# Mixer A's values by Strassen's seven products, ahead of its attention, in a two-layer encoder on one core

## The chip, the cores and the metric

The kernel runs on one core of one Trainium2 chip. The metric is the device time of one execution, in microseconds (us); lower is better. The kernel before takes 1451.28 us in the median of 3 runs (1450.83 to 1451.67). The profile is one more execution: 1451.78 us, of which 1449.6 us lie between its first and its last instruction.

Five engines work beside each other, each through its own instructions in a fixed order: TensorE (PE in the profile; its weight loads are PEld), VectorE (DVE), ScalarE (ACT), GpSimd (POOL), and SyncE (SP), which only issues transfers. An engine stops at an instruction whose semaphores have not arrived, and everything behind it on that engine stops too.

## The reference

Two layers on x (512 positions of 1024 numbers, float32). Each layer is x = x + mixer(norm(x)), then x = x + mlp(norm(x)), with mlp(h) = relu(h·w1)²·w2 over 4096 hidden columns. Layer 0's mixer, the one that the change touches:

```python
def dilated_mixer(h, w_qkv, q_gain, k_gain, w_o):
    qkv = (h @ w_qkv).reshape(B, S, 3, N_GROUPS, A_HEADS, A_HEAD_DIM)   # 3 groups, 8 heads of 128
    outs, lses = [], []
    for g, (window, dil) in enumerate(DIL_CONFIGS):     # (128, 1), (512, 4), (2048, 16)
        q = rope(rms_norm(qkv[:, :, 0, g], q_gain[g]), S)
        k = rope(rms_norm(qkv[:, :, 1, g], k_gain[g]), S)
        v = qkv[:, :, 2, g]
        o, lse = dilated_group(q, k, v, window, dil)    # softmax over a dilated window
        outs.append(o); lses.append(lse)
    wts = jax.nn.softmax(jnp.stack(lses, 0), axis=0)
    o = wts[0][..., None] * outs[0]
    for g in range(1, N_GROUPS):
        o = o + wts[g][..., None] * outs[g]
    return o.reshape(B, S, A_WIDTH).astype(h.dtype) @ w_o
```

The values v are thus a plain product of h (512 x 1024) with 3 groups x 8 heads x 128 = 3072 columns of w_qkv. Layer 1 uses multi-head latent attention, which the change does not touch.

## The kernel before

**Matmuls in three passes.** Every float32 operand of a large product is split into a high part (rounded by ACT, `whi` for weights) and a low part (the difference, by DVE, `wlo`), and a product is hi·hi + hi·lo + lo·hi: three matmuls of 128 x 128 by up to 512 columns each. `load_unit` (L145 to L159) loads a piece of weights of 256 rows (`raw`, by SP, L146 or L148), and splits it (ACT L157, DVE L158). `run_block` (L161 to L190) holds the results of four row tiles of 128 positions in four PSUM banks and goes through the units of weights in groups: `[1] * 4` takes one unit at a time for all four tiles, `[4]` all units for one tile and then the next. The matmul is L184. Four pairs of `whi` and `wlo` buffers are shared by the whole program.

**Norm and turn.** `norm_tile` (L204 to L221) scales a tile of x by its root mean square (ACT's square L136, a power on POOL L131, DVE L212) and a gain, turns it by eight transposes on TensorE (L123), and splits it into `hT`.

**Mixer A.** Four pairs of heads, one after the other. For each pair `qk_block` projects queries and keys of group 0, 1 and 2 (512 columns, 192 matmuls each), normalises and rotates them (squares on ACT, then DVE L308, L311, L315, L316), turns them, and computes scores and exponentials (L340 to L362). Then `v_all` runs twice, once per head: `v_block` projects the values of the head's three groups together (384 columns, 96 matmuls of 128x384); group 0's part makes a round trip through DRAM into another order (`v0n`, `v0c`). `merge` (L376 to L417) weighs the three groups, and `pv` (L419 to L446) multiplies with the values. In the last pair one head's values come ahead of the queries and keys. Then `project` (L635) multiplies with `w_o`, after splitting the heads' outputs (L655).

**MLP.** The product with w2 goes in four chunks of 1024 rows; each is a Strassen product (Winograd's form) with seven half-sized products instead of eight: `wino` (L489 to L590). Weight sums are made by transfers that POOL issues and that add to what is in the buffer (accumulates, L509); sums of activations by DVE (L517), split at L485 and L486; the matmul is L580. The table `ORDER` (L588) sets the products' order: 1, 5, 3, 6, 2, 7, 4. Each product takes 24 matmuls of 512 columns.

**What sets the order.** The program is written in the order above, but a scheduler lays each engine's instructions out beforehand by its own estimate of when their inputs are ready: matmuls of one product can be put between those of another. On the chip each engine then keeps that order.

## Time and profile before

| | |
|---|---|
| median of 3 runs | 1451.28 us (1450.83 to 1451.67) |
| the profiled execution | 1451.78 us |
| its span, first to last instruction | 1449.6 us |
| TensorE busy | 1410.4 us, 97% |
| VectorE, ScalarE, GpSimd busy | 887.1, 727.2, 198.4 us |
| moved by SP's queue, by POOL's accumulates | 142.74 MB, 33.56 MB |
| mean granted clock of TensorE | 0.999 |

How to read it: a row of a timeline gives start, duration, engine, line, operation, output<-input with shapes, and in brackets the engine's idle time ahead of it with what ended it. A group's row gives the count, then busy time and the mean in ns, then idle time and its releasers. Durations of matmuls are latencies and overlap; the interval at which they follow each other is read from their starts. A wait row gives what the engine waited for, the total in us, how often, and the longest.

### The profile page before, as it was taken

Reading aid. Unit: us, or ns where it says so; the run is one execution under the profiler, and the core shown is the slowest. Engines: PE = TensorE matmul, PEld = TensorE weight load, DVE = VectorE, ACT = ScalarE, POOL = GpSimd, SP = SyncE. Lnnn points to the kernel's source line nnn. Section 1 sums busy time; section 2 is a strip of 40 time slices with the busy share of each in tenths; the row PEclk is TensorE's granted clock in tenths of the full one; section 3 lists DMA queues with packets and bytes.
Section 4 is the critical chain, followed back from the end, with each engine's and each line's share of the span. In section 5 each row is a group of like instructions: output and inputs, shape, how many; then the busy total and the mean of one; then the engine's idle time right before and its main releaser. Section 6 shows DMA issues by size and latency. Waiting matters only on the chain.

```text
span 1449.6 us, 19315 instructions
## 1 busy us (share of the span) xinstructions
PE 1410.4 (97%) x7116; PEld 1196.8 (83%) x7116; DVE 887.1 (61%) x1421; ACT 727.2 (50%) x1590; POOL 198.4 (14%) x197
## 2 busy tenths in 40 slices
PE   7999999999999999999999999899999999999998
PEld 6889889889988878888888877776768988888877
DVE  6765566566537655266475749788755266475647
ACT  5544455355335533453544545777633454544543
POOL 1120120011011101011020222332101011020210
PEclk9999999999999999999999999999999999999999
DMA  7325114321622344749394853310013749394853
GB/s 228 100 57 162 58 49 129 110 63 45 174 92 62 97 140 141 222 112 236 91 233 127 195 136 66 99 30 30 30 44 136 206 111 239 93 223 138 189 116 88
DMA packets 134813, 177.52 MB, mean 122 GB/s; under 512 B 8768, under 2 KB 73536, under 8 KB 134720
## 3 DMA queue, kind: packets, MB, share of 16 engines
q1 hardware_dynamic: 117312, 142.74, 31.1%
q0 software_dynamic: 17408, 33.56, 14.0%
q8 instruction: 56, 0.92, 0.2%
q14 instruction: 37, 0.30, 0.1%
HBM read 172.07 MB, written 4.19 MB: 122 GB/s over the span
## 4 chain that ended last, share of the span: by engine, by line
PE 89%; ACT 4%; DVE 3%; DMA 2%; issue 1%; POOL 1%; SPq 0%; DVEq 0%; ACTq 0%; POOLq 0%
PE acc L184 58%; PE sc L580 10%; PE tp L580 7%; PE tp L123 4%; PE acc L859 1%; PE acc L835 1%; PE sc L753 1%; PE sco L444 1%; PE sco L440 1%; PE sc L351 1%; PE sc L835 1%; ACT whi L157 1%; ACT junkb L136 1%; DVE wlo L158 1%; PE tp L859 0%
## 5 line engine op out<-in xcount | busy, mean ns | idle before, releaser
L184 PE MATMUL acc<-whi,hT 128*128 128x512 f32 (+2 forms) x1600 | 486.3, 379 | 5.6 <-DVE t L311 2.2
L158 DVE TENSOR_TENSOR wlo<-raw,whi 128x1024 fp32r<-128x1024 f32 (+3 forms) x170 | 195.7, 1156 | 230.5 <-ACT whi L157 229.5
L184 PEld LDWEIGHTS acc<-whi,hT 128*128 128x128 f32 x1600 | 296.2, 189 | 47.3 <-issue 2.9
L184 PE MATMUL acc<-hT_f,whi 128*128 128x512 f32 (+1 forms) x1152 | 319.4, 366 | 1.9 <-DVE resid L641 1.2
L157 ACT ACTIVATE whi<-raw 128x1024 fp32r<-128x1024 f32 (+3 forms) x170 | 170.0, 1005 | 269.0 <-PE acc L184 177.4
L184 PE MATMUL acc<-wlo,hT 128*128 128x512 f32 (+2 forms) x800 | 300.2, 375 | 0.2 <-DVE wlo L158 0.2
L184 PEld LDWEIGHTS acc<-hT_f,whi 128*128 128x128 f32 x1152 | 208.4, 189 | 37.8 <-DVE resid L641 1.6
L524 DVE TENSOR_TENSOR wlo<-wqs,whi 128x1024 fp32r<-128x1024 f32 x112 | 137.3, 1227 | 113.6 <-ACT whi L523 113.5
L184 PE MATMUL acc<-hT_f,wlo 128*128 128x512 f32 (+1 forms) x576 | 205.1, 365 | 0.0
L523 ACT ACTIVATE whi<-wqs 128x1024 fp32r<-128x1024 f32 x112 | 118.6, 1060 | 167.6 <-PE acc L184 66.2
L184 PEld LDWEIGHTS acc<-wlo,hT 128*128 128x128 f32 x800 | 151.2, 189 | 20.5 <-DVE wlo L158 1.1
L580 PE MATMUL sc<-whi,asp 128*128 128x512 f32 x512 | 165.1, 390 | 0.8 <-ACT asp L485 0.8
L509 POOL DMA_DIRECT2D wqs<-in_ffn_w_dram x64 | 77.6, 1350 | 528.4 <-DVE wlo L524 339.9
L184 PEld LDWEIGHTS acc<-hT_f,wlo 128*128 128x128 f32 x576 | 108.6, 189 | 17.5
L131 POOL TENSOR_TENSOR qrs<-rs_v,nhalf 128x4 f32<-128x4 f32 x48 | 61.5, 1290 | 408.3 <-DVE rs_v L128 393.8
L580 PE MATMUL tp<-whi,asp 128*128 128x512 f32 x352 | 112.2, 390 | 2.6 <-DVE asp L486 2.6
L580 PEld LDWEIGHTS sc<-whi,asp 128*128 128x128 f32 x512 | 96.1, 188 | 21.6 <-ACT asp L485 1.6
L580 PE MATMUL sc<-wlo,asp 128*128 128x512 f32 x256 | 99.6, 389 | 0.0
L580 PEld LDWEIGHTS tp<-whi,asp 128*128 128x128 f32 x352 | 65.9, 188 | 17.2 <-DVE asp L486 3.5
L580 PE MATMUL tp<-wlo,asp 128*128 128x512 f32 x176 | 68.5, 389 | 0.0
L136 ACT ACTIVATE junk<-acc 128x128 f32<-128x128 f32 x192 | 53.1, 277 | 18.9 <-PE acc L184 13.8
L554 DVE TENSOR_TENSOR resid<-resid,sc 128x512 f32<-128x512 f32 x64 | 43.0, 682 | 24.4 <-PE sc L580 24.4
(190 smaller groups left out, 1796.3 us busy)
## 6 DMA issues: line engine op xcount, KB each, us to landing
wqs<-in_ffn_w_dram SPq DMA_DIRECT2D x80, 512.0 KB, 5.1
raw<-in_ffn_w_dram SPq DMA_DIRECT2D x64, 512.0 KB, 4.4
wqs<-in_ffn_w_dram POOLq DMA_DIRECT2D x64, 512.0 KB, 7.2
raw<-in_a_w_qkv_dram SPq DMA_DIRECT2D x96, 256.0 KB, 3.4
raw<-in_a_w_qkv_dram SPq DMA_DIRECT2D x64, 192.0 KB, 2.8
raw<-in_a_w_o_dram SPq DMA_DIRECT2D x8, 512.0 KB, 4.0
raw<-in_b_w_o_dram SPq DMA_DIRECT2D x8, 512.0 KB, 3.7
xt<-in_x_dram SPq DMA_DIRECT2D x8, 256.0 KB, 5.7
```

Source lines behind the costliest of these rows:

```text
L123: PE.transpose(o, i, ident)
L131: G.tensor_tensor(out, v[:, :n], nhalf[:, :n], op=ALU.pow)
L136: A.activation(junk, x, AF.Square, scale=1.0 / math.sqrt(dim), accum_out=out)
L157: A.activation(hi[:, :nk, :n], raw[:, :nk, :n], AF.Copy)
L158: V.tensor_tensor(lo[:, :nk, :n], raw[:, :nk, :n], hi[:, :nk, :n].bitcast(F32), op=ALU.subtract)
L184: PE.matmul(accs[o][:, oc], lhsT=lt, rhs=rt, start=(kt == 0 and p_i == 0 and hv == 0), stop=(kt == total - 1 and p_i == 2), skip_group_che ...
L509: nc.gpsimd.dma_start(t, src, accum_op=ALU.add)
L523: A.activation(hi, x, AF.Copy)
L524: V.tensor_tensor(lo, x, hi.bitcast(F32), op=ALU.subtract)
L554: V.tensor_tensor(sl, sl, banks[t], op=op)
L580: PE.matmul(bk[t], lhsT=lt, rhs=rt[:, j], start=(first and k == 0 and i_ == 0), stop=(k == 3 and i_ == 2), skip_group_check=True)
L835: PE.matmul(sc, lhsT=lt, rhs=rt, start=(i == 0), stop=(i == 4))
```

## The change

**Values first.** The work on the values of six heads moves ahead of the attention into a new function `v_phase`. For each group these heads' 768 columns, the 1024 rows and the 512 positions are halved, and seven products take the place of eight: 24 matmuls of 128x384 each. Products of unsummed halves (2 and 1) come first; for group 0 the head numbered 6 is then projected directly, while DVE and ACT make and split the sums of activations (`Ssp`); then 5, 3, 6, 7, 4 (`piece`). The weight operand `bT` is b11 + b12 (DVE), becomes b11 + b12 + b22 for product 6 and that plus b21 for product 4 through accumulates on POOL's queue (L331: 12 transfers of 384 KB). The results go to DRAM (`vall`), and each pair of heads reads its part back (`v_load`). The gain is loaded ahead of x.

**Attention.** The blocks of queries and keys follow one another without values between them, in groups of two units (`[2, 2]`). A pair's softmax end, merge and product with the values stand behind the first block of the next pair. The last head (7) is projected directly behind the last scores (`v_last`), and the first column block of `w_o` is begun between the last two heads' `pv` (`first_cols`).

**MLP.** In the last chunk of each layer the products run in the order 1, 2, 5, 3, 6, 7, 4 (`ORDER_LAST`).

The diff, cut to its core:

```diff
@@ -237,95 +244,322 @@
+        def add_block(t, g, ki, ni):
+            for u in range(2):
+                nc.gpsimd.dma_start(t[:, 2 * u:2 * u + 2], wblk(g, ki, ni, u), accum_op=ALU.add)
...
+        gain_b = gain_table(norm_mix[0:1, :].rearrange("o d -> (o d)"), D, "g_mix0")
+        load_x(0)
+        nc.sync.dma_start(ck[:, 0:P], consts[:, 0:P])
+        b21[0] = block(0, 1, 0, "b21")
+        load_x(1)
+        b11[0] = block(0, 0, 0, "b11")
+        load_x(2)
+        load_x(3)
...
+        def product(p, w, banks, first, u, t):
+            if (p, u) not in parts:
+                split(p, w, u)
+            hi, lo = parts[p, u]
+            for j in range(2):
+                k = 2 * u + j
+                ah, al = A_OF[p](k, 0, t), A_OF[p](k, 1, t)
+                for i_, (lt, rt) in enumerate(((ah, hi), (ah, lo), (al, hi))):
+                    PE.matmul(banks[t][:, :VH], lhsT=lt, rhs=rt[:, j], start=(first and k == 0 and i_ == 0),
+                              stop=(k == 3 and i_ == 2), skip_group_check=True)
...
+        def piece(g, ba):
+            bb = new_banks("b")
+            both(5, bT[g], bb, True)
+            put(g, 1, 1, "set", bb, False)
+            add_block(bT[g], g, 1, 1)
+            both(3, b22[g], bb, False)
+            put(g, 0, 1, "set", bb, False)
+            b3 = vp.tile([P, 4, VH], F32, tag="h32", name=nm("b3"))
+            for u in range(2):
+                us = slice(2 * u, 2 * u + 2)
+                V.tensor_tensor(b3[:, us], b12[g][:, us], b22[g][:, us], op=ALU.add)
+            both(6, bT[g], ba, False)
+            put(g, 0, 1, "sub", ba, True)
+            add_block(bT[g], g, 1, 0)
+            both(7, b3, ba, False)
+            put(g, 1, 1, "sub", ba, True)
+            both(4, bT[g], ba, False)
+            put(g, 1, 0, "set", ba, True)
...
+            both(2, b21[g], bd, True)
+            put(g, 0, 0, "set", bd, False)
+            both(1, b11[g], ba, True)
+            put(g, 0, 0, "add", ba, True)
+            for u in range(2):
+                sum1(g, u)
+            piece(g, ba)
...
+        for b in range(HA // 2):
...
+            vs = v_load(b)
+            for g in range(NG):
+                scores(b, g, qkT, Pt, stats)
+                if g + 1 < NG:
+                    qkT = project_in(b, g + 1)
+            if b + 1 < HA // 2:
+                qkT = project_in(b + 1, 0)
+                finish(b, Pt, stats, vs)
...
+        merge(stats, Pt)
+        v_last(*vs)
+        oA = new_hT()
+        for h in range(HA - 2):
+            split_o(h)
+        pv(HA // 2 - 1, 0, Pt, *vs)
+        first_cols = block_groups(w_units(a_w_o[0], 0, 512), [3, 1], 512, act_stationary(oA, 512))
+        next(first_cols)
+        pv(HA // 2 - 1, 1, Pt, *vs)
...
-        for p, chain, first, (i, n, op) in ORDER:
+        for p, chain, first, (i, n, op) in ORDER if done is None else ORDER_LAST:
...
+    ORDER_LAST = [ORDER[0], ORDER[4]] + ORDER[1:4] + ORDER[5:]
```

**The order on the engines.** First TensorE in the new V phase, group 0: the end of product 5 (operand `Ssp`, banks `tp`), the first two matmuls of product 6 (banks `sc`, weights `whi_549` from the accumulated `bT`), and then product 3.

```order
L422 MATMUL tp_483<-wlo_465,Ssp_111 128x384
L422 MATMUL tp_483<-whi_464,Ssp_111 128x384 x2
L422 MATMUL tp_483<-wlo_465,Ssp_111 128x384
L422 MATMUL tp_483<-whi_464,Ssp_111 128x384
L422 MATMUL sc_157<-whi_549,Ssp_112 128x384 [waits Activation_49]
L422 MATMUL sc_158<-whi_549,Ssp_112 128x384
L422 MATMUL tp_482<-whi_512,Ssp_114 128x384 [waits Activation_49]
L422 MATMUL tp_482<-wlo_513,Ssp_114 128x384 [waits DVE_49]
```

Nothing of this stood here before; product 3 can start only behind the two matmuls of product 6, whose weights wait for the accumulate.

Then POOL at layer 0's last w2 chunk: `wqs` are the chunk's weight buffers (an accumulate each), `cgB` and `sgB` are tables for layer 1. Before:

```order
L509 DMA wqs_5335<-in_ffn_w_dram 128x2x512 [waits DMASW6_49,DVE_49]
L691 TENSOR_TENSOR cgB<-ck,gr 128x4x32 [waits DMAHW6_49,PE_49]
L692 TENSOR_TENSOR sgB<-ck,gr 128x4x32
...
L691 TENSOR_TENSOR cgB<-ck,gr 128x4x32 [waits DMAHW7_49]
...
L509 DMA wqs_5335<-in_ffn_w_dram 128x2x512 [waits DMASW7_49,DVE_49]
L693 TENSOR_SCALAR sgB<-sgB 128x8x32 [waits Pool_49]
L509 DMA wqs_5335<-in_ffn_w_dram 128x2x512 [waits DMASW4_49,DVE_49]
```

And now:

```order
L966 TENSOR_TENSOR cgB<-ck,gr 128x4x32 [waits DMAHW0_49,PE_49]
L967 TENSOR_TENSOR sgB<-ck,gr 128x4x32
...
L966 TENSOR_TENSOR cgB<-ck,gr 128x4x32 [waits DMAHW1_49]
...
L968 TENSOR_SCALAR sgB<-sgB 128x8x32 [waits Pool_49]
L779 DMA wqs_5372<-in_ffn_w_dram 128x2x512 [waits DMASW2_49,DVE_49]
L779 DMA wqs_5372<-in_ffn_w_dram 128x2x512 [waits DMASW3_49,DVE_49]
```

The rows left out are more `cgB` and `sgB` operations: nine in all, the last one being `sgB<-sgB`. Of product 6's two accumulates the first stood ahead of the nine and the second behind eight of them; now both stand behind all nine.

Last TensorE at the same place now: the end of product 5 (banks `tp_7493` and `tp_7494`, operand `asp_7490`), two matmuls of product 6 (`sc`, operand `asp_7571`), then product 3.

```order
L850 MATMUL tp_7494<-wlo_7512,asp_7490 128x512
L850 MATMUL tp_7494<-whi_7511,asp_7490 128x512
L850 MATMUL sc_7411<-whi_7574,asp_7571 128x512 [waits Activation_49]
L850 MATMUL sc_7412<-whi_7574,asp_7571 128x512
L850 MATMUL tp_7493<-whi_7535,asp_7532 128x512 [waits DVE_49]
L850 MATMUL tp_7493<-wlo_7536,asp_7532 128x512
```

Two matmuls of product 6 stand ahead of product 3, as four did before; their weights come from the first of the two accumulates.

More of the change, by code (lines that the diff above doesn't have):

```diff
@@ L174, in run_block @@
                 src, nk, dims = units[ui]
-                loaded.append(load_unit(src, nk, dims, n, (name, ui)))
+                loaded.append(load_unit(src, nk, dims, n, raw=raws[ui] if raws else None))
                 ui += 1
@@ L188, in run_block @@
                     if gi == len(groups) - 1 and hv == halves - 1:
-                        evac(o, accs[o])
+                        yield o, accs[o]
             kt0 = nkt
+            if gi < len(groups) - 1:
+                yield None
+    def run_block(units, groups, n, mm, evac, outs=NT, halves=1):
+        for end in block_groups(units, groups, n, mm, outs, halves):
+            if end is not None:
+                evac(*end)
     def act_stationary(hT, n):
@@ L643, in evac @@
                     norm_tile(r, resid[:, r], gain, hT_n, pool)
+            if c == 0 and begun is not None:
+                for end in begun:
+                    if end is not None:
+                        evac(*end)
+                continue
             run_block(w_units(w, 512 * c, 512), [1, 1, 1, 1] if c == 0 else [4], 512, act_stationary(o_hl, 512), evac)
```

381 lines of the change are left out of this document (266 added, 115 removed).

## The prediction

> **What bounds the kernel now.** I read the page first (who is busy), then TensorE's waits (what its idle time is made of), then a table by stage, and timelines where a stage is touched.
>
> ```profile
> PE 1410.4 (97%) x7116; PEld 1196.8 (83%) x7116; DVE 887.1 (61%) x1421; ACT 727.2 (50%) x1590; POOL 198.4 (14%) x197
> ...
> q1 hardware_dynamic: 117312, 142.74, 31.1%
> q0 software_dynamic: 17408, 33.56, 14.0%
> ```
>
> TensorE is busy for 1410.4 of 1449.6 us. So work taken from it shortens the run one for one, as long as the others keep up, and only 39 us of waiting can be gained or added to. TensorE's waits, with the total, the number and the longest:
>
> ```profile
> PE tp L123 <- DVE xn L212: 9.9, 2, 8.9
> PE tp L580 <- DVE asp L486: 2.6, 2, 1.5
> PE tp L123 <- DVE pT L426: 2.4, 2, 2.1
> PE acc L184 <- DVE t L311: 2.2, 1, 2.2
> PE sc L580 <- ACT asp L485: 0.8, 2, 0.4
> ```
>
> The first row is the start (8.9 us until the first norm is done); the others lie in places that the change touches. By stage (the first 60 us of QK blocks, one pair of heads in steady state, the last pair, the start of w_o):
>
> ```profile
> 30.00:93.00 63.00, 61.43 (x311) 51.38 (x309) 44.69 (x86) 37.08 (x127) 12.70 (x10) 1.00 0.23 69
> ...
> 150.24:273.92 123.68, 123.65 (x702) 111.42 (x702) 75.14 (x143) 60.48 (x190) 14.74 (x12) 1.00 0.30 90
> ...
> 395.84:527.00 131.16, 127.72 (x700) 111.89 (x700) 80.12 (x150) 64.91 (x196) 15.56 (x12) 1.00 0.29 90
> 527.00:580.00 53.00, 50.45 (x311) 44.02 (x310) 26.13 (x36) 17.01 (x27) 4.63 (x6) 1.00 0.42 148
> ```
>
> After the length come TensorE, its weight loads, DVE, ACT and POOL. A steady pair leaves TensorE 0.03 us idle in 123.68: a pure TensorE stage.
>
> **The change part by part.** The sum is made against the profiled execution, 1451.78 us.
>
> *Fewer products.* A V matmul at full and at half clock:
>
> ```profile
> 91.04 0.39 PE L184 MATMUL acc<-whi,hT 128*128 128x512 f32 x1
> 93.67 0.41 PE L184 MATMUL acc<-whi,hT 128*128 128x384 f32 x1 [2.24 <-DVE t L311]
> ...
> 94.09 0.51 PE L184 MATMUL acc<-whi,hT 128*128 128x384 f32 x2
> 94.44 0.33 PE L184 MATMUL acc<-wlo,hT 128*128 128x384 f32 x1
> 94.61 0.51 PE L184 MATMUL acc<-whi,hT 128*128 128x384 f32 x2
> ...
> 96.18 1.16 PE L184 MATMUL acc<-whi,hT 128*128 128x384 f32 x3
> 97.14 0.52 PE L184 MATMUL acc<-wlo,hT 128*128 128x384 f32 x1
> ```
>
> From 94.09 to 94.61 three are issued: 0.173 us each. (0.33 is latency, not the interval.) Six heads took 6 x 96 = 576 such matmuls; three groups by seven products by 24 are 504. **72 x 0.173 = -12.5 us.** All else on TensorE keeps its count.
>
> *The stall at 91.4.* It stood where V's first matmul wanted a bank that QK's evacuation still held; now no V block follows. It cost 2.24 us, and behind it the clock fell: from 96.18 to 97.14 three matmuls take 0.96 us, 0.32 each, for some 3.2 us, of which (0.32 - 0.173)/0.32 = 1.5 is lost. **-3.7** (0 if the same wait comes back behind a QK block).
>
> *The start.* Now the gain is loaded ahead of x, and x's first tile comes last of the two.
>
> ```profile
> 8.87 1.97 PE L123 MATMUL tp<-ck,xn 128*128 128x128 f32 x8 [8.87 <-DVE xn L212]
> 10.97 0.79 PE L184 MATMUL acc<-whi,hT 128*128 128x512 f32 x1
> ```
>
> ```profile
> 4.51 1.06 ACT L136 ACTIVATE xn<-xt 128x1024 f32<-128x1024 f32 x1 [2.28 <-DMA xt<-in_x_dram]
> ```
>
> ```profile
> 7.53 1.29 DVE L212 SCALAR_TENSOR_TENSOR xn<-xt,nrs,g_mix 128x1024 f32<-128x1024 f32 x1 [1.68 <-DMA g_mix<-in_norm_mix_dram]
> ```
>
> ```profile
> L131 POOL TENSOR_TENSOR qrs<-rs_v,nhalf 128x4 f32<-128x4 f32 x48 | 61.5, 1290 | 408.3 <-DVE rs_v L128 393.8
> ```
>
> x's first tile landed at 4.4 and the gain at 7.4, 3.0 later. With the gain first both have landed at 7.4, but the square (4.51 to 5.7), POOL's power (1.3) and the scaling (1.29) follow x: the scaling would end at 4.4 + 1.3 + 1.3 + 1.3 = 8.3 if only x were waited for, so 3.0 later, at 11.3, now: 2.5 later than the 8.82 of before. One half of the columns is enough for product 2, so only four transposes of the eight (1.97) stand ahead: first matmul near 13.1 instead of 10.97. **+2.1** (+1 to +5: the later tiles of x queue behind 768 KB weight blocks, but 48 matmuls, 8.3 us, of products 2 and 1 cover them).
>
> *The V phase's own waits.* Per group, product 5's operand bT becomes product 6's by a POOL accumulate, and product 6's first two matmuls stand ahead of product 3 in TensorE's order. Accumulates, splits and their prices:
>
> ```profile
>   ACT whi L523: 11.8, 6
> ...
> DMA to landing us min/median/max: 6.0/7.2/14.3
> ```
>
> ```profile
> L158 DVE TENSOR_TENSOR wlo<-raw,whi 128x768 fp32r<-128x768 f32 x8 | 7.6, 955 | 9.9 <-ACT whi L157 9.8
> L157 ACT ACTIVATE whi<-raw 128x768 fp32r<-128x768 f32 x8 | 6.8, 848 | 7.6 <-PE acc L184 6.7 <-DMA raw<-in_a_w_qkv_dram 0.6 <-PE sc L351 0.2
> ```
>
> A product is 24 x 0.173 = 4.16 us; call the start of product 2 zero. Four split buffers are shared, so bT's first half can be split when product 2 has used its first half, at 2.1; ACT 0.85, DVE 0.96: the accumulate goes out at 3.9. Product 6 is wanted behind 2, 1 and 5, at 12.5, and needs ACT's 0.85 first: a landing of up to 7.7 us is free. The 512 KB ones took 7.2 in the median and these are 384 KB. DVE's sums (two per group, like a split each) can hold the split up by 1 to 2 us. Traffic: some 20 MB of plain transfers at 142.74 MB per 31.1% of 1449.6 us (63 us) and 4.7 MB accumulated at 33.56 MB per 14.0% (28 us), 91 us in a phase of 600 x 0.173 = 104: the queues are rarely empty. Best 0 (landings near 6.0); worst, at 12 us each, 4.3 + 1.5 of half clock three times, 17. I take **+2.0**, nearest the median row. The second accumulate (product 4's) has product 7 more for cover. For a price that only a page states: the Trainium skill, "DMA: Bandwidth & Descriptors", section "Anatomy of one DMA", puts a DMA from GpSimd at 2.0 us plus its bytes over 436 KB per us, 2.9 us here; by it this term is 0 and the sum 2 lower. The trace's fastest, 6.0 for 512 KB where the rule says 3.2, disagrees.
>
> *QK blocks without V beside them.* A pair loses 192 x 0.173 = 33.3 us of TensorE and, on DVE, eight splits (7.6): DVE has 75.14 - 7.6 = 67.5 us in 123.68 - 33.3 = 90.4, 75%. The window 30 to 93 is just that, QK blocks back to back with DVE at 71%, and there TensorE was idle for 1.57 us, all of it the stall at 91.43. Groups of two units let the four banks finish 12 matmuls (2.7 us) apart. Softmax, merge and P·V of a pair now lie in the next pair's blocks. **+1.5** over four pairs (0 to +15, a stall like the one at 91.4 in each).
>
> *End of mixer A.* The table's last rows hold 3.4 and 2.6 us of idle. The last head and the begun w_o block cover part: **-1.0** (0 to -2.5).
>
> *Product 2 second in each layer's last down chunk.* Layer 0:
>
> ```profile
> 860.05 0.39 PE L580 MATMUL sc<-whi,asp 128*128 128x512 f32 x1
> ...
> 865.49 0.39 PE L580 MATMUL tp<-whi,asp 128*128 128x512 f32 x1
> ...
> 868.06 0.73 PE L580 MATMUL tp<-whi,asp 128*128 128x512 f32 x2 [1.50 <-DVE asp L486]
> ...
> 873.32 0.50 PE L580 MATMUL sc<-whi,asp 128*128 128x512 f32 x1 [0.43 <-ACT asp L485]
> ```
>
> Product 1 takes 5.44 us; product 5 stalls 1.50 for its operand, and 0.43 comes at the next change. Product 2's operand needs no subtraction, so both go: -1.9. But product 2 also takes two split buffers, and so bT's first half, split by 857 before, is split only after product 1's first half. Its accumulate for product 6 loses its place on POOL:
>
> ```profile
> 864.01 1.08 POOL L691 TENSOR_TENSOR cgB<-ck,gr 128x128 f32<-128x128 f32 x1 [5.60 <-DMA gr<-in_b_q_gain_dram]
> ...
> 871.50 1.44 POOL L692 TENSOR_TENSOR sgB<-ck,gr 128x128 f32<-128x128 f32 x1
> 872.89 1.19 POOL L509 DMA_DIRECT2D wqs<-in_ffn_w_dram  x1
> 873.68 1.55 POOL L693 TENSOR_SCALAR sgB<-sgB 128x256 f32<-128x256 f32 x1
> 875.20 1.26 POOL L509 DMA_DIRECT2D wqs<-in_ffn_w_dram  x1
> ```
>
> In the changed order all nine cgB and sgB operations stand ahead of both accumulates. Eight end at 872.9, the ninth 1.55 later: the first accumulate goes out at 874.4, lands 6.0 to 7.2 later, and ACT needs another 1.06 (the row below): 881.5 to 882.7. TensorE wants it at 860.05 + 3 x 5.44 = 876.4, since product 6's first two matmuls stand ahead of product 3. Stall 5.1 to 6.3, taken 5.4, and half clock 1.5 behind it.
>
> ```profile
> L523 ACT ACTIVATE whi<-wqs 128x1024 fp32r<-128x1024 f32 x112 | 118.6, 1060 | 167.6 <-PE acc L184 66.2
> ```
>
> Layer 0: -1.9 + 5.4 + 1.5 = **+5.0** (-1.9 to +7). Layer 1 has no such operations on POOL; of the waits' rows 2.6 - 1.5 = 1.1 and 0.4 go: **-1.5**.
>
> Sum: -12.5 - 3.7 + 2.1 + 2.0 + 1.5 - 1.0 + 5.0 - 1.5 = **-8.1**, so 1443.7 for an execution like the profiled one; the runs' median lies 0.5 below it: **1443.2 us**.
>
> **The rivals.** *Product 6 of layer 0 isn't late* (the start of the nine operations comes earlier, or the scheduler's order leaves product 3 room). Then that term is -1.9: 1443.2 - 6.9 = 1436.3. For it: POOL sits idle for 5.60 us before the nine, waiting for gr alone. Against: gr waits for TensorE's last use of the memory it takes, the same instant as before.
>
> *The accumulates bound the V phase.* Each group stalls once where a landing exceeds 7.7 us; with the clock's 1.5, landings of 12 give 3 x (4.3 + 1.5) = 17.4 in place of 2.0: 1458.6, slower. For it: 14.3 us was seen, 11.8 us of waits for them are on the page's list, and the queues are nine tenths full. Against: the median. It is slower than before from (8.1 + 2.0)/3 = 3.4 us per group, 1.9 without the clock, a landing of 9.6. On the clock: the 2.24 us gap was followed by half speed; the Trainium skill, "TensorE: Matmul & The Clock Gate", section "Why this matters for your kernels", allows gaps up to about 3 us. By that rule 1.9 us gaps cost no 1.5 and this rival turns slower only from a landing of 11.1; the trace halved after less.
>
> *DVE falls behind without V.* A stall as at 91.4, 2.24 + 1.5, once per QK block of the later three pairs: 9 x 3.7 = 33; once per pair, 15: 1443.2 - 1.5 + 15 = 1456.7. It turns slower from three such stalls. For it: merge and P·V now lie beside QK evacuations. Against: 60 us without a stall at 71%.
>
> **How the numbers follow.** The forecast, 1439 to 1448, 0.55; layer 0 not late (1433 to 1439) 0.20; accumulates 0.13; DVE 0.12. A measurement tells 0.2%, 2.9 us, from no change: faster is below 1448.4, slower above 1454.2. Faster: nearly all of the first two, and a fifth of the others (stalls of half the size), 0.79; no change 0.09; slower 0.12. The range runs from the second case's middle to half-sized stalls in the last two: 1435 to 1452.
>
> **What would show it.** 792 matmuls of 384 columns; first matmul near 13; in the V phase gaps under 1.5 us ahead of product 6, waiting for ACT; no wait for t in the QK blocks; a gap of about 5 us at product 6 of layer 0's last chunk with half clock behind it, and the accumulate issued right behind the ninth POOL operation; none at layer 1's. The forecast is wrong if the V phase runs at half clock, or if the QK blocks show waits for DVE.

## The result, and the profile after

The changed kernel takes 1441.68 us in the median of 4 runs (1438.60 to 1444.44), the kernel before 1451.05 us in 4 runs beside them (1450.07 to 1451.67): a ratio of 0.9937, with a 95% interval of 0.9918 to 0.9957. The same program taken again with the first experiments gave 1444.54 us (1440.63 to 1445.45, 5 runs) and 0.9948 (0.9936 to 0.9961). The forecast, 1443.2 us, lies between the two medians. The profiled execution is the shortest of the nine, 1438.6 us; so a second profile of the same program, of a run of 1445.45 us, is read beside it and called the second execution below.

The head of the page of the changed kernel:

```profile
span 1436.8 us, 19234 instructions
...
PE 1398.5 (97%) x7044; PEld 1184.7 (82%) x7044; DVE 928.6 (65%) x1485; ACT 746.6 (52%) x1626; POOL 213.0 (15%) x209
...
q1 hardware_dynamic: 106848, 150.47, 32.8%
q0 software_dynamic: 20672, 38.28, 16.2%
```

TensorE has 72 instructions fewer (7044 against 7116) and 11.9 us less busy time. What it paid with: DVE 41.5 us more, and 4.7 MB more through the accumulates' queue. TensorE's waits in the changed kernel:

```profile
PE tp L123 <- DVE xn L362: 10.5, 1, 10.5
PE sc L850 <- ACT whi L793: 4.7, 1, 4.7
...
PE sc L422 <- ACT whi L407: 1.9, 2, 1.5
...
PE sc L422 <- DVE vo L441: 1.2, 2, 1.0
...
PE tp L850 <- DVE resid L824: 0.9, 1, 0.9
```

The wait for `t` that stood in the QK blocks (2.2 us) is gone, and the one for `pT` at the end of mixer A (2.4 us) is down to 0.3. In their place stand the waits of the V phase (L422) and one of 4.7 us in the MLP (L850). By stage, in the columns length, TensorE, weight loads, DVE, ACT, POOL, granted clock, DMA share and GB/s:

```profile
16.03:47.91 31.88, 30.81 (x181) 29.32 (x180) 29.36 (x44) 19.13 (x34) 4.42 (x4) 1.00 0.83 250
47.91:116.00 68.09, 64.66 (x365) 62.88 (x365) 42.31 (x53) 33.84 (x50) 12.03 (x10) 1.00 0.74 184
...
206.00:296.00 90.00, 90.00 (x511) 77.65 (x510) 65.24 (x132) 49.46 (x173) 13.42 (x11) 1.00 0.30 94
...
847.00:892.00 45.00, 40.20 (x174) 32.61 (x173) 38.80 (x41) 24.66 (x30) 17.06 (x15) 0.96 0.34 59
```

The QK blocks (third row) leave TensorE idle for nothing that two digits show, with DVE at 72%. DVE is at 92% in the first row, most of group 0 in the V phase. TensorE's losses are in the first two rows (1.1 and 3.4 us) and in the last (4.8 us). The two places of the forecast, in the timeline of TensorE: product 6 of group 0 in the V phase, and product 6 of layer 0's last w2 chunk.

```profile
49.40 0.62 PE L422 MATMUL sc<-whi,Ssp 128*128 128x384 f32 x2 [1.48 <-ACT whi L407]
...
868.83 1.22 PE L850 MATMUL sc<-whi,asp 128*128 128x512 f32 x2 [4.73 <-ACT whi L793]
869.84 0.63 PE L850 MATMUL tp<-whi,asp 128*128 128x512 f32 x1
870.27 0.63 PE L850 MATMUL tp<-wlo,asp 128*128 128x512 f32 x1
```

And POOL at the second place:

```profile
850.85 0.54 POOL L966 TENSOR_TENSOR cgB<-ck,gr 128x128 f32<-128x128 f32 x1 [26.59 <-DMA gr<-in_b_q_gain_dram]
...
859.36 1.71 POOL L968 TENSOR_SCALAR sgB<-sgB 128x256 f32<-128x256 f32 x1
861.03 2.50 POOL L779 DMA_DIRECT2D wqs<-in_ffn_w_dram  x2
```

The nine operations on the tables run from 850.85 to 861.0, the accumulates go out right behind the ninth, ACT's split follows at 867.7, and TensorE starts again at 868.83, at half clock (0.43 us from matmul to matmul, where 0.23 is usual).

Where the 12.8 us of span went (1449.6 to 1436.8), by two instants that both traces have: up to the first matmul of layer 0's MLP (567.20 before, 554.76 now) -12.4; from there to a projection of queries early in layer 1's attention, ahead of which TensorE waits 2.0 us in both (936.30, 926.33), +2.5; from there to the end -2.8.

### The profile page after: what moved, and what is told of

Its sections match the earlier page's. It is cut to its first block, busy times and chain, and to the rows that moved or that the text cites. A ratio compares the mean times of both kernels' runs of the same rounds, so it can differ in the third digit from the quotient of the medians.

```text
span 1436.8 us, 19234 instructions
## 1 busy us (share of the span) xinstructions
PE 1398.5 (97%) x7044; PEld 1184.7 (82%) x7044; DVE 928.6 (65%) x1485; ACT 746.6 (52%) x1626; POOL 213.0 (15%) x209
## 4 chain that ended last, share of the span: by engine, by line
PE 87%; DMA 4%; ACT 3%; DVE 3%; issue 1%; POOL 1%; SPq 0%; ACTq 0%; DVEq 0%; POOLq 0%
PE acc L184 51%; PE sc L850 11%; PE tp L850 8%; PE tp L123 4%; PE sc L422 2%; PE acc L1134 1%; PE acc L1110 1%; PE sc L1028 1%; DMA b<-in_a_w_qkv_dram 1%; PE sco L699 1%; PE sc L585 1%; PE sco L695 1%; PE tp L422 1%; DMA bT<-in_a_w_qkv_dram 1%; DMA raw<-in_a_w_qkv_dram 1%
## 5 line engine op out<-in xcount | busy, mean ns | idle before, releaser
L184 PE MATMUL acc<-whi,hT 128*128 128x512 f32 (+2 forms) x1216 | 383.2, 389 | 2.8 <-ACT hT L737 1.3
L157 DVE TENSOR_TENSOR wlo<-raw,whi 128x1024 fp32r<-128x1024 f32 (+3 forms) x146 | 172.2, 1187 | 172.5 <-ACT whi L156 171.9
L184 PEld LDWEIGHTS acc<-whi,hT 128*128 128x128 f32 x1216 | 225.8, 188 | 44.0 <-ACT hT L737 1.9
L156 ACT ACTIVATE whi<-raw 128x1024 fp32r<-128x1024 f32 (+3 forms) x146 | 149.5, 1031 | 177.2 <-PE acc L184 83.8
L184 PE MATMUL acc<-wlo,hT 128*128 128x512 f32 (+2 forms) x608 | 236.0, 389 | 0.7 <-DVE wlo L157 0.7
L850 PE MATMUL sc<-whi,asp 128*128 128x512 f32 x512 | 165.6, 391 | 4.9 <-ACT whi L793 4.7
L184 PEld LDWEIGHTS acc<-wlo,hT 128*128 128x128 f32 x608 | 114.4, 188 | 19.4 <-DVE wlo L157 1.0
L850 PEld LDWEIGHTS sc<-whi,asp 128*128 128x128 f32 x512 | 96.2, 188 | 25.9 <-ACT whi L793 5.2
L850 PE MATMUL tp<-whi,asp 128*128 128x512 f32 x352 | 112.8, 392 | 0.9 <-DVE resid L824 0.9
L850 PE MATMUL sc<-wlo,asp 128*128 128x512 f32 x256 | 99.6, 389 | 0.0
L850 PEld LDWEIGHTS tp<-whi,asp 128*128 128x128 f32 x352 | 66.7, 190 | 15.3 <-DVE resid L824 1.3
L850 PE MATMUL tp<-wlo,asp 128*128 128x512 f32 x176 | 68.7, 392 | 0.0
L824 DVE TENSOR_TENSOR resid<-resid,sc 128x512 f32<-128x512 f32 x64 | 43.1, 681 | 26.3 <-PE sc L850 26.3
```

What stands on the lines that cost most here:

```text
L156: A.activation(hi[:, :nk, :n], raw[:, :nk, :n], AF.Copy)
L157: V.tensor_tensor(lo[:, :nk, :n], raw[:, :nk, :n], hi[:, :nk, :n].bitcast(F32), op=ALU.subtract)
L184: PE.matmul(accs[o][:, oc], lhsT=lt, rhs=rt, start=(kt == 0 and p_i == 0 and hv == 0), stop=(kt == total - 1 and p_i == 2), skip_group_che ...
L824: V.tensor_tensor(sl, sl, banks[t], op=op)
L850: PE.matmul(bk[t], lhsT=lt, rhs=rt[:, j], start=(first and k == 0 and i_ == 0), stop=(k == 3 and i_ == 2), skip_group_check=True)
```

## The experiments

Each is the changed kernel with one or more edits, and runs of the kernel before stand beside it on the same chip; ratios are to these. "Against 0.9948" compares with the ratio of the changed kernel among the first four. The runs of the first four, of the next four, and of the three behind them (the later read back, and two of the combinations) share a chip each; the changed kernel itself ran beside the first four alone. The second execution is the profile of the first:

> The changed kernel as it is, to be compared with the others on the same chip. Its four runs so far lie between 1438.6 and 1444.4 us, wider than the 1.6 us of the kernel before, and the longer ones have the lower mean clock (0.997, 0.996, 0.995). Theory: the gaps of 1 to 2 us that the V phase has are followed by half clock in some executions and not in others, so the spread repeats, some 4 to 6 us wide, with the time rising as the mean clock falls. Rival: the spread is the chip's, then the kernel before shows as much here.

Its five runs spread over 4.8 us, where the fifteen of the kernel before lie within 3.1, and the shortest has the highest mean clock (0.996, the others 0.995): the spread repeats, as expected. It matters for everything below. In group 0 and at the change to group 1 TensorE waits 1.24, 1.22 and 1.79 us there, and it runs at half clock from 51.7 to 55.1 and from 65.4 to 68.8 us, which the first profile doesn't show at all. Each such stretch loses about 1.7 us (the sum of one minus the granted clock over its microseconds). Up to the MLP the second execution is 5.4 us behind the first (560.11 against 554.76).

The wait of 1.79 us is the one that varies most: 1.01 in the first profile (at 61.79), 2.80 in the run with layer 0's order below, none above 0.25 in the best combination. TensorE waits there for a sum on DVE that empties a bank (`vo`). That sum stands behind another in DVE's order, one of group 1's weights, and DVE sits idle until these weights have landed. The two sums, in the first profile and in the second execution:

```profile
60.31 0.96 DVE L461 TENSOR_TENSOR b<-b,b 128x768 f32<-128x768 f32 x1 [1.16 <-DMA b<-in_a_w_qkv_dram]
61.19 0.55 DVE L441 TENSOR_TENSOR vo<-vo,sc 128x384 f32<-128x384 f32 x1
```

```profile
63.00 0.96 DVE L461 TENSOR_TENSOR b<-b,b 128x768 f32<-128x768 f32 x1 [1.93 <-DMA b<-in_a_w_qkv_dram]
63.88 0.55 DVE L441 TENSOR_TENSOR vo<-vo,sc 128x384 f32<-128x384 f32 x1
```

SP issued that piece of weights at 51.16 and 51.73; it landed 9.1 and 11.2 us later, where such transfers take 6.2 in the median. DVE's idle time and TensorE's wait go together in the other traces with this order of work: 2.12 and 2.80, 1.91 and 1.75, 0.48 and 0.34, 0.19 and none. The wait of 1.24 us is a landing's too: ACT is idle for 1.89 us until weights of head 6 have come.

One thing has to be known ahead of the comparisons. The scheduler lays the whole program out anew for each edit, so a stage that no edit touches can change. The lengths of four stages in us, one profiled execution each: up to the first matmul of layer 0's MLP; from there to the first query projection of layer 1; from there to the first matmul with layer 1's output weights, which is layer 1's attention; and the rest.

| profile | to the MLP | to layer 1's queries | layer 1's attention | rest |
|---|---|---|---|---|
| kernel before | 567.20 | 359.66 | 147.63 | 375.07 |
| changed, first | 554.76 | 362.32 | 145.92 | 373.85 |
| changed, second | 560.11 | 362.64 | 146.11 | 373.84 |
| layer 0 order | 558.17 | 359.56 | 145.94 | 373.90 |
| tables later | 558.82 | 364.72 | 145.92 | 373.85 |
| eight half products | 560.53 | 361.96 | 147.71 | 375.32 |
| x first | 559.68 | 363.00 | 147.46 | 375.04 |
| single units | 562.01 | 362.86 | 148.04 | 375.42 |
| sum by DVE | 559.37 | 362.83 | 147.99 | 375.76 |
| read back later | 555.02 | 362.40 | 145.78 | 373.83 |
| layer 0 order, x first, DVE's sum | 555.44 | 358.49 | 147.64 | 374.68 |
| and the later read back | 556.86 | 359.13 | 147.50 | 374.41 |
| and the gain first | 554.77 | 359.19 | 147.96 | 374.63 |
| layer 0 order and later read back | 554.07 | 359.18 | 145.66 | 375.38 |

Layer 1's attention has two lengths, 145.7 to 146.1 and 147.5 to 148.0. In the six traces of the first kind TensorE's instructions stand in one order there, the same in all six. In the others it is another; in all of these but the eight half products it is that of the kernel before. So 1.5 to 1.7 us of the change's gain come from an order that the scheduler happened to make, and the experiments on the eight half products, x, the single units and DVE's sum lose them again, whatever their edits do. The rest differs by up to 2 us as well; a stretch of half clock near 1100 us is in four of the traces (eight half products, single units, DVE's sum, the last row), and what else it holds stays open.

**The order in layer 0's last chunk.** `ORDER` there, `ORDER_LAST` in layer 1 alone:

```diff
-        for p, chain, first, (i, n, op) in ORDER if done is None else ORDER_LAST:
+        for p, chain, first, (i, n, op) in ORDER_LAST if done is not None and tag >= 4 else ORDER:
```

> Only layer 0's last down chunk goes back to the order 1, 5, 3, 6, 2, 7, 4; layer 1 keeps 1, 2, 5, 3, 6, 7, 4. Theory: the order costs 5 us at layer 0, because product 6's first accumulate stands behind nine table operations on GpSimd. Then the 4.73 us gap at product 6 and the half clock behind it (1.4 us lost) go, gaps of about 1.5 and 0.4 us at products 5 and 6 come back, and the time is 4 us under the changed kernel's, about 1437.5. Rival: the gap only moves to another product of the chunk; then it is within 1 us of the changed kernel.

Measured: 1439.56 us (1437.48 to 1442.71), 0.9919 (0.9907 to 0.9932), against 0.9948 for the changed kernel: 4.2 us saved. The stage that has the chunk is 2.8 to 3.1 us shorter in the table. POOL in this run:

```profile
848.17 1.20 POOL L779 DMA_DIRECT2D wqs<-in_ffn_w_dram  x1 [20.55 <-DVE wlo L794]
854.75 1.30 POOL L966 TENSOR_TENSOR cgB<-ck,gr 128x128 f32<-128x128 f32 x1 [5.38 <-DMA gr<-in_b_q_gain_dram]
...
862.46 1.44 POOL L967 TENSOR_TENSOR sgB<-ck,gr 128x128 f32<-128x128 f32 x1
863.84 1.19 POOL L779 DMA_DIRECT2D wqs<-in_ffn_w_dram  x1
```

The first accumulate is ahead of the tables again. TensorE's gaps there are 1.49 and 0.39 us, as in the kernel before (1.50 and 0.43), and no half clock follows. So the order of products in this one chunk costs 3 to 4 us, for the reason forecast: product 2's split comes ahead of the split that frees the accumulate's place on POOL.

**The tables later instead.** A copy on DVE into the tables' source `gr` makes their load wait, so that the nine operations come behind product 6's accumulates, with `ORDER_LAST` kept:

```diff
             gr = bp.tile([P, 2, RD], F32, name="gr")
+            V.tensor_copy(gr[:, :, 0], resid[:, 0, 0:2])
```

> The changed kernel's order in both layers, but the gain that the nine table operations need is loaded only after product 2's sum (a copy of two numbers of the residual into its tile stands ahead of the load), so that both accumulates of product 6 stand ahead of the nine on GpSimd. Theory: the cause is GpSimd's order, not product 2's place; the gap of 4.73 us shrinks below 1 us and neither of the old gaps (1.50 and 0.43 us) comes back, so 6 us under the changed kernel, about 1436. Rival: it is the split buffers, which product 2 holds; then the first accumulate still goes out late and more than 3 us of gap stay.

Measured: 1446.11 us (1445.20 to 1448.77), 0.9964 (0.9952 to 0.9977): no gain, if anything 2 us lost (the table's second stage is 2.1 to 2.4 us longer than the changed kernel's). The stall went from product 6 to product 4. POOL and, behind it, DVE in this run:

```profile
862.29 1.20 POOL L779 DMA_DIRECT2D wqs<-in_ffn_w_dram  x1 [1.67 <-DVE wlo L794]
870.85 0.45 POOL L967 TENSOR_TENSOR cgB<-ck,gr 128x128 f32<-128x128 f32 x1 [7.35 <-DVE wlo L794]
...
880.12 1.19 POOL L779 DMA_DIRECT2D wqs<-in_ffn_w_dram  x1
...
881.73 1.73 POOL L779 DMA_DIRECT2D wqs<-in_ffn_w_dram  x1
```

```profile
887.26 1.23 DVE L794 TENSOR_TENSOR wlo<-wqs,whi 128x1024 fp32r<-128x1024 f32 x1 [6.22 <-ACT whi L793]
888.40 0.68 DVE L824 TENSOR_TENSOR resid<-resid,sc 128x512 f32<-128x512 f32 x1
```

Product 6's accumulates now go out in time (859.42 and 862.29). But the tables take 10 us of POOL wherever they stand, and the next two accumulates, product 4's, wait behind them until 880.12 and 881.73. ACT can split only at 886.17, DVE's split stands ahead of the sum that empties a bank (L824), and TensorE waits 4.95 us. A place for the tables would have to be one with 10 us free of accumulates; this edit only changed who stands behind them.

**Eight half products in place of seven.** The V phase without sums: each quarter of the result as two plain products, no accumulates, no sums of activations or weights. It leaves out the Strassen part of the change and computes the same values:

```diff
-            both(5, bT[g], bb, True)
-            put(g, 1, 1, "set", bb, False)
-            add_block(bT[g], g, 1, 1)
...
+            both(32, b21[g], bb, True)
+            both(31, b11[g], bb, False)
+            put(g, 1, 0, "set", bb, True)
...
```

> The V phase at its new place, but with eight half-sized products per group in place of seven and without any sums of activations or weights (no accumulates in mixer A). All else as changed. Theory: 72 matmuls of 0.173 us come back, 12.5 us, and the V phase's gaps at product 6 (1.5, 1.0 and 0.5 us) go, so 9.5 us over the changed kernel, about 1451, where the kernel before is: the reordering alone (the stall at 91.4 gone, the later start, the 4.73 us gap) is worth nothing in sum. Rival: the gain came from the reordering of the attention and the seven products are paid back by their own waits; then it is within 3 us of the changed kernel.

Measured: 1448.39 us (1446.61 to 1449.13, 11 runs), 0.9980 (0.9971 to 0.9989): 3.9 us slower than the changed kernel on the same chip, not the 9.5 expected. By the table 3.1 to 3.3 of that lie behind the first query projection of layer 1, where the edit changes nothing but the scheduler's order. So the total doesn't price the products; the first stage does, for the executions that were profiled. This trace has no gap above 0.25 us in the V phase and no half clock there, and its MLP starts at 560.53. In the four traces with the changed kernel's V phase and read back the MLP starts at 554.76, 560.11, 558.17 and 558.82. So of the 12.5 us that 72 matmuls are worth, the seven products kept 5.8, 0.4, 2.4 and 1.7.

In the second execution nearly all of the 12.5 us went back, of which the rows name about 10: 5.2 us of gaps, two stretches of half clock (3.4), and 1.8 us in the first QK block (below) against 0.4 here. In the first, with 3.9 us of gaps and no half clock, they kept most.

It also shows what the rest of the change is worth. Without Strassen the MLP starts 6.7 us ahead of the kernel before (560.53 against 567.20), which is more than the seven products added in any of the four. Over the whole run, with the loss in layer 0 still in it, 0.2%, or 2.9 us, are left.

**x ahead of the gain.**

```diff
-        gain_b = gain_table(norm_mix[0:1, :].rearrange("o d -> (o d)"), D, "g_mix0")
         load_x(0)
+        gain_b = gain_table(norm_mix[0:1, :].rearrange("o d -> (o d)"), D, "g_mix0")
```

> The changed kernel with x's first tile loaded ahead of the gain, as the kernel before does. Theory: the start costs what the first transposes are later, 10.54 - 8.87 = 1.7 us, and this comes back: ratio to the kernel before 0.001 lower than the changed kernel's 0.9948, about 1443. Rival: the V phase runs at the pace of its transfers (the fourth weight piece of the first head and the accumulates), so that a start 1.7 us earlier only makes the gaps behind it longer: no difference.

Measured: 1446.85 us (1444.84 to 1449.05), 0.9968 (0.9955 to 0.9980): some 3 us slower than the changed kernel by the ratios (whose intervals overlap a little), not faster. The table puts 2.6 to 2.7 of that into layer 1, which x doesn't touch; up to the MLP it takes 559.68, between the changed kernel's two executions. TensorE's waits in this run:

```profile
PE tp L123 <- DVE xn L362: 9.1, 1, 9.1
PE sc L422 <- ACT whi L407: 5.7, 2, 4.0
```

The start is 1.4 us shorter than in the first profile, and product 6 of group 0 waits 4.0 instead of 1.5, with 6.8 us of half clock behind it (from 49.5 on). The accumulate goes out at 43.33, where the changed kernel issues it at 42.97 and 43.57: DVE and ACT, which prepare it, had nothing of the earlier start, and this landing took a little longer (ACT's split at 50.26 against 48.50 and 48.84). TensorE only arrived sooner at a wait. Here the earlier start was worth nothing, since the next operand was bound elsewhere.

**QK blocks in single units.**

```diff
-        run_block(qk_units(b, g), [2, 2], 512, act_stationary(hT, 512),
+        run_block(qk_units(b, g), [1] * 4, 512, act_stationary(hT, 512),
```

> The changed kernel with its query and key blocks in groups of one unit, [1, 1, 1, 1], as before, in place of [2, 2]. Theory: without values between the blocks, groups of two are what lets VectorE keep up; with ones the four banks finish within 5 us of each other and a wait as at 91.4 us (2.2 us and 1.7 us of half clock) comes at some of the 11 block changes: 10 to 40 us slower, 1455 to 1485. Rival: VectorE's 75% is enough either way; within 3 us of the changed kernel.

Measured: 1450.70 us (1446.69 to 1452.64, 10 runs), 0.9992 (0.9981 to 1.0003): 6.4 us slower than the changed kernel by the ratios, not the 10 to 40 expected. By the table 3.5 to 3.7 of these lie in layer 1. TensorE waits for the evacuation of a bank at the starts of two QK blocks (the longer of the two 2.5 us):

```profile
PE acc L184 <- DVE rs_v L128: 4.2, 2, 2.5
```

The longer one, at 152.4, stands where the second execution waits 1.79 us for late weights (below). The other, 1.73 us at 207.9, is new: neither profile of the changed kernel waits there, and no weights are late. The squares on ACT that empty the banks start only at 206.56 there, behind eight exponentials. This wait is of the kind that stood ahead of the old V block, so it isn't tied to V. It fits the theory of four banks that finish together, but it is one wait of one trace, and no run takes it apart.

**Product 6's sum by DVE.** In `piece`:

```diff
-            add_block(bT[g], g, 1, 1)
+            for u in range(2):
+                us = slice(2 * u, 2 * u + 2)
+                V.tensor_tensor(bT[g][:, us], bT[g][:, us], b22[g][:, us], op=ALU.add)
```

> The changed kernel, with b22 (which lies in a buffer anyway) added to bT for product 6 by VectorE, two operations of 128x768 a group, in place of the accumulate; product 4's accumulate stays. Theory: the V phase gives back 6 to 10 of the 12.5 us because the landing of the first accumulate sets product 6, and the second, queued behind it, product 7 and 4 through VectorE's fixed order; then the gaps at product 6 go, and with them most of the half clock: 4 us or more under the changed kernel's 1444.5, ratio to the kernel before 0.992 or less. Rival: VectorE, 62 to 92% busy in this phase, is what is late; six operations of 0.95 us more make it worse: 1 to 4 us slower.

Measured: 1445.14 us (1443.05 to 1447.72), 0.9953 (0.9940 to 0.9967), against 0.9948: nothing gained, though the table's last two stages again take 3.8 to 4.0 us more. The gap at product 6 is gone in all three groups. At the change from group 0 to group 1 three others stand in its place. TensorE's timeline in this run:

```profile
61.88 0.62 PE L422 MATMUL acc<-whi,hT 128*128 128x384 f32 x2 [1.17 <-ACT whi L407]
...
64.15 0.44 PE L422 MATMUL sc<-whi,hT 128*128 128x384 f32 x1 [1.64 <-DVE vo L441]
...
67.62 0.44 PE L422 MATMUL acc<-wlo,hT 128*128 128x384 f32 x1 [1.10 <-DVE wlo L408]
```

What ACT did ahead of the first of them:

```profile
60.25 0.84 ACT L407 ACTIVATE whi<-bT 128x768 fp32r<-128x768 f32 x1 [3.05 <-DMA bT<-in_a_w_qkv_dram]
```

ACT was idle for 3.05 us until product 4's accumulate had landed, and the split that TensorE waits for stands behind that. Ahead of the sum for the second gap DVE was idle too, 2.85 us for the same split on ACT and 0.58 us for weights of group 1; only ahead of the third does it work without a pause. So the rival, a DVE that is late with its own work, explains one gap in three. Taking one landing away moved TensorE's wait to the next landings.

**The values read back later.** In the first pair `v_load` (11 transfers that SP issues) moves from ahead of the QK blocks to behind the next block in the program:

```diff
-            vs = v_load(b)
+            vs = v_load(b) if b else None
...
                     qkT = project_in(b, g + 1)
+                if vs is None:
+                    vs = v_load(b)
```

> The changed kernel with one edit: the first pair's values are read back from DRAM (11 transfers, 2.1 MB) behind that pair's second and third query and key block in the program and not ahead of its first, so that the first block's third and fourth weight pieces go out on SP ahead of most of them. Theory: the gap at 150 to 155 us (1.2 to 3.0 us, in some executions with 1.7 us of half clock) is the first query and key block waiting for weights that stand on SP behind the read back, which itself waits for the V phase's last results; it goes, 1 to 4 us under the changed kernel: ratio to the kernel before 0.992 to 0.994. Rival: it is VectorE, which makes rotation tables at 133 to 139 us; then the gap stays.

It came out of the second execution. At 153.55 TensorE waits 1.79 us for a bank of the second QK block, where the first profile waits 0.17. SP's queue there:

```profile
133.10 0.60 SPq L625 DMA_DIRECT2D vt<-vall  x1
...
136.27 7.33 SPq L604 DMA_DIRECT2D v0c<-vall  x8
143.64 0.60 SPq L625 DMA_DIRECT2D vt<-vall  x1
144.34 10.19 SPq L144 DMA_DIRECT2D raw<-in_a_w_qkv_dram  x10
```

The read back takes SP from 133.1 to 144.2, and the weights of the QK blocks (`raw`) wait behind it. What that does on ACT, in the same run:

```profile
149.56 1.06 ACT L156 ACTIVATE whi<-raw 128x1024 fp32r<-128x1024 f32 x1 [9.16 <-DMA raw<-in_a_w_qkv_dram]
151.30 1.06 ACT L156 ACTIVATE whi<-raw 128x1024 fp32r<-128x1024 f32 x1 [0.68 <-DMA raw<-in_a_w_qkv_dram]
152.26 0.26 ACT L136 ACTIVATE junk<-acc 128x128 f32<-128x128 f32 x1
```

ACT idles 9.16 us for weights, and the squares that empty the first block's banks start only at 152.26, behind the late splits. The values are multiplied only behind the next pair's first block. With the read back later in the program, SP issues its transfers from 132.6 on between the weights; that split comes at 143.66 and TensorE has no gap; the two windows from 132 to 160, first of the second execution and then of this experiment:

```profile
132.00:160.00 28.00, 26.14 (x120) 21.20 (x118) 15.65 (x26) 11.59 (x38) 3.81 (x3) 1.00 0.72 218
```

```profile
132.00:160.00 28.00, 28.00 (x129) 23.20 (x128) 21.74 (x38) 12.78 (x39) 4.82 (x4) 1.00 0.77 231
```

Measured: 1439.62 us (1437.27 to 1442.57, 6 runs), 0.9922 (0.9906 to 0.9938), against 0.9948 on the other chip: 3.8 us, with intervals that overlap a little. The windows show 1.9 us of it where the edit works.

**Together.** Four combinations: the layer 0 order, x first and DVE's sum; the same with the later read back; that one with the gain first; and the layer 0 order with the later read back alone. The edits are the ones shown; of the last, whole:

```diff
-            vs = v_load(b)
+            vs = v_load(b) if b else None
...
+                if vs is None:
+                    vs = v_load(b)
...
-        for p, chain, first, (i, n, op) in ORDER if done is None else ORDER_LAST:
+        for p, chain, first, (i, n, op) in ORDER_LAST if done is not None and tag >= 4 else ORDER:
```

> Three edits at once: layer 0's last down chunk in the old order, b22 added by VectorE, x's first tile loaded first. If the three causes are separate their savings add up: 5 (the order, measured) + 4 or more (the accumulate) + 0 to 1.7 (the start): 1434 to 1436. If the V phase is bound by VectorE: 1438 to 1442.

> Four edits: layer 0's last down chunk in the old order, b22 added by VectorE, x's first tile first, and the later read back. If the last edit adds to the other three: 1 to 2 us under their 1438.0 (ratio 0.9909), about 1436.5, ratio 0.9895 to 0.990.

> The same with the gain ahead of x, as in the change. Theory: the start is worth its 1.7 us only where nothing behind it waits for transfers; with the accumulate for product 6 gone it is, so this one is 1 to 2 us slower than the one with x first. Rival: it made no difference, or a loss, in the changed kernel, and makes none here.

> Two edits to the changed kernel: layer 0's last down chunk in the old order and the later read back of the first pair's values; the accumulates and the gain stay where the change has them. If the two causes are separate places, their savings add up: 4 to 5 us each under the changed kernel's ratio of 0.9948, so 0.9885 to 0.990, about 1435, and this beats all the others. If the earlier work only moves later waits: about 1438, as the versions with four edits.

| kernel | median (lowest to highest) | ratio to before, 95% |
|---|---|---|
| layer 0 order, x first, DVE's sum | 1437.97 (1436.47 to 1440.31) | 0.9909 (0.9896 to 0.9923) |
| and the later read back | 1438.02 (1435.41 to 1440.72) | 0.9910 (0.9894 to 0.9925) |
| and the gain first | 1438.10 (1437.95 to 1438.32) | 0.9910 (0.9896 to 0.9924) |
| layer 0 order and later read back | 1436.22 (1435.41 to 1437.37) | 0.9896 (0.9879 to 0.9912) |

With DVE's sum the place of x makes no difference, and the later read back adds nothing: a gap of 1.25 us at 149.44 goes, and one at 62 us grows from 1.62 to 2.70, with DVE idle ahead of it for weights (0.55 us, then 1.64). The lowest median has the pair of edits that only take away what the runs had shown to be a loss. It beats both kernels: 14.9 us under the one before, and 0.5% under the changed one by the ratios. Against the other three its interval overlaps, and it alone has the shorter order in layer 1's attention, by 1.8 to 2.3 us, which is as much as lies between the medians (1.8); so whether DVE's sum itself gains or loses isn't shown. TensorE's waits in the pair (the layer 0 wait of 4.7 us is gone, the one of the V phase for `vo` is 0.2):

```profile
PE tp L123 <- DVE xn L362: 10.8, 1, 10.8
...
PE sc L422 <- ACT whi L407: 1.4, 1, 1.4
```

## Why the prediction was right

The sign, the size and most places were forecast; four terms were mis-sized (the V phase above all), 1.5 us came from a stage that the sum didn't have, and the total was right partly by luck, because errors of both signs met. The terms of the sum in the forecast, the profiled execution, and the second one where it differs (gaps above 0.25 us, and half clock at 1.7 us a stretch):

| term | forecast | first profile | second |
|---|---|---|---|
| fewer products | -12.5 | -12.5 (72 instructions fewer) | |
| the stall at 91.4 and its half clock | -3.7 | gone, -3.9 | gone |
| the start | +2.1 | +1.5 (first V matmul at 12.48, not 10.97) | +1.1 |
| the V phase's own waits | +2.0 | +3.9 | +8.6 |
| QK blocks without V | +1.5 | 0 | +1.8, from SP's queue |
| end of mixer A | -1.0 | -2.9 (4.5 us of gaps became 1.6) | -2.9 |
| layer 0's last chunk | +5.0 | +4.5 | +5.0 |
| layer 1's last chunk | -1.5 | -0.5 | -0.5 |
| layer 1's attention | none | -1.7 | -1.5 |

Up to the MLP the forecast's terms add up to -11.6, and the two executions gave -12.4 and -7.1. The first profile's entries for these terms add up to -13.9 where -12.4 was measured; 1.5 us of loss has no row of its own.

*Fewer products* came as worked out from the 0.173 us interval. *The stall and the QK blocks*: right in kind, and a little too careful. Four pairs back to back keep TensorE at 90.00 of 90.00 us with DVE at 72%; the rival of a DVE that falls behind found no row in the first profile. What looks like it in the second, a wait for `rs_v`, was late weights, and goes when SP's queue is put right.

*The V phase's waits* is the step that failed. It was priced by the landing of product 6's accumulate alone: with up to 7.7 us free and a median near 7.2, little would be left. These landings were as hoped. The group's median by the page of the profile, the first issue on POOL, and the split that follows the landing on ACT:

```profile
bT<-in_a_w_qkv_dram POOLq DMA_DIRECT2D x12, 384.0 KB, 6.1
```

```profile
42.97 2.67 POOL L331 DMA_DIRECT2D bT<-in_a_w_qkv_dram  x2 [19.88 <-DVE wlo L408]
```

```profile
48.50 0.84 ACT L407 ACTIVATE whi<-bT 128x768 fp32r<-128x768 f32 x1 [3.31 <-DMA bT<-in_a_w_qkv_dram]
```

In group 1 the time line held: the accumulate went out 7.5 us ahead of TensorE (73.31 against 80.81), and 0.47 us of wait were left. But in group 0 it went out only at 42.97, where TensorE was through with product 5 at 47.91: 4.9 us ahead, not the 8.6 of the forecast (12.5 less 3.9). The forecast's "2, 1 and 5" leaves out that head 6's projection stands between products 1 and 5 there, with four splits of weights and the sums of activations beside it. DVE is at 92% in that window, and the weights' split that releases the accumulate is taken up without a pause ahead of it:

```profile
41.70 0.95 DVE L408 TENSOR_TENSOR wlo<-bT,whi 128x768 fp32r<-128x768 f32 x1
```

The largest of DVE's groups there is

```profile
L388 DVE TENSOR_TENSOR Ssp<-dif,Ssp 128x512 fp32r<-128x512 f32 x7 | 4.7, 684 | 0.1
```

the splits of the sums of activations, which only the first group has. ACT's part of the split ended at 41.58, just ahead, so both engines would have had to be earlier. "DVE's sums can hold the split up by 1 to 2 us" was in the working, and not in the term.

That is 1.8 of the 3.9 us in the first profile and 1.5 of the 5.2 us of gaps in the second. Of the others, 1.0 in the first profile and 3.0 in the second (1.24 and 1.79) are waits that the term didn't have, for plain weights behind which other work stood in an engine's fixed order. The rival in which the accumulates bound the phase needed landings above 7.7 us at product 6; in the two profiles the first half of its weights, which is the one that TensorE waits for, landed after 5.2 to 7.0 in every group. What landed late were weights of the next group (9.1 and 11.2 us) and, in the run with DVE's sum, product 4's accumulate. Against the one trace of the eight half products, 6.7 to 12.1 us of the 12.5 had been given back by the MLP in four executions (12.5 less 5.8, less 0.4). For a price that only a page states: the Trainium skill, "DMA: Bandwidth & Descriptors", section "Anatomy of one DMA", gives an estimate of 2.9 us for such a transfer; the trace's median of 6.1 disagrees, and the forecast had gone by rows.

*Layer 0's last chunk* came in its place, its mechanism and nearly its size: 4.73 of stall and 1.7 of half clock, less the 1.9 us that the new order saves; the run with the old order takes 4.2 us back. The stage as a whole is 2.7 to 3.0 us longer than before. The rival in which product 6 is not late falls. Of the loss 1.0 us seems to return at once: the kernel before waits 1.01 us at 895.37 for the norm of the next layer, and the changed kernel has no such gap. *Layer 1* gained 0.5 instead of 1.5: the two waits for `asp` go (1.13 and 0.33), and a new one of 0.92 us comes, because product 5 now finds its bank still being emptied (`resid`, L824); the forecast had named no rival for that bank. *Not in the sum*: 1.5 to 1.7 us gained in layer 1's attention (147.63 us before, 145.92 and 146.11 now). The table of stages shows where they come from: the order in which the scheduler laid that stage out, which the runs with the order of before lose again.

What stays open beside it: the rest of the V phase's spread. The traces tell which landings and splits TensorE waits for, not why one piece of weights took 9 us in one execution and 11 in another, nor why half clock follows a gap in one and not in the other.

## What to carry to other kernels

A product fewer is worth its matmuls less what its operands cost: look at how busy DVE is in the stage where the sums fall, and at what else stands in the engines' fixed orders behind a transfer, not only at how long the one transfer takes to land. When the order of products changes, follow what each split releases on the queue of the accumulates, since a run of ten microseconds of small operations there delays whatever is put behind it. And at a change of stage read the order of SP's queue: results read back early stand ahead of weights that are wanted now. Before two versions are compared by their totals, compare their stages: where a scheduler lays the program out anew, a stage that nobody touched can move by more than the edit is worth.

## What the runs showed of the hardware

Half clock came behind shorter waits than I had reckoned with, and not always. In the second execution a gap of 1.22 us and one of 0.28 us behind it are followed by this window (the granted clock is the third number from the end):

```profile
52.00:55.00 3.00, 3.00 (x11) 3.00 (x10) 0.96 (x1) 1.33 (x2) 0.24 (x2) 0.50 0.99 330
```

In the first execution gaps of 1.48 and 0.28 us stand at the same instructions, and the clock stays at 1.00. The Trainium skill, "TensorE: Matmul & The Clock Gate", section "Why this matters for your kernels", warns of gaps above about 3 us; here 1.5 us in all, within 2.1 us, went with a drop. That page's section "Part 1: The HAM clock gate (the "warmup" mystery)" describes a free-running window of activity of 3413 ns; that the same program sometimes drops and sometimes doesn't agrees with it, and so does the length of the stretches: in all fourteen traces each one that ends before the run does lasts 3.41 us or twice that. No run here shows where a window begins.

Half clock isn't always a loss either. Ahead of a query projection of layer 1 (936.30 and 926.33) both kernels wait 2.0 us. The five microseconds behind that wait, first before, then in the changed kernel:

```profile
936.00:941.00 5.00, 3.73 (x21) 3.02 (x22) 3.82 (x17) 4.97 (x25) 3.57 (x5) 1.00 0.02 3
```

```profile
926.00:931.00 5.00, 4.67 (x20) 4.43 (x20) 3.50 (x17) 4.80 (x22) 3.55 (x5) 0.66 0.00 0
```

At a clock of 1.00 TensorE is busy for 3.73 us, at 0.66 for 4.67, and about as many matmuls start (21 and 20): ACT is busy nearly throughout (4.97 and 4.80), and the slow matmuls fill what was idle. That ACT sets the pace is read from these rows, not tried. But what the half clock cost can be read from two traces in which all engines have the same order in layer 1's attention: the run with layer 0's order alone has the stretch (1.7 us lost) and takes 145.94 us for that stage, the pair of edits has none and takes 145.66.
